# Attention of a hybrid decoder step on one core: TensorE in program order, two transpose banks, projections bank by bank at their ends

## The chip, the cores and the metric

The kernel runs on one core of one Trainium2 chip. The metric is the device time of one execution in microseconds (us), from the first to the last instruction with what lies around it; the median of several executions is quoted. Inside a core five engines work side by side, each through its own list of instructions in a fixed order: TensorE (PE, with its weight loads as PEld), VectorE (DVE), ScalarE (ACT), GpSimd (POOL) and SyncE (SP), which here only issues transfers. They wait for one another through semaphores. Matmul results land in PSUM, which has eight banks of 128 x 512 floats.

## The reference

One inference step of a two-layer trunk: 1024 prompt tokens and 8 sample tokens (1032 columns in the kernel), model width 1024. Layer 0 is a recurrent block, layer 1 is sliding-window attention, and each is followed by a squared-ReLU MLP of width 4096. The change lies in layer 1:

```python
def qkv_heads(x, w_qkv, q_g, k_g):
    q, k, v = jnp.split(x @ w_qkv, [Q_DIM, Q_DIM + KV_DIM], axis=-1)   # 16 query heads, 4 key/value heads of 64
    q = rms_norm(q.reshape(n, t, N_KV, GROUP, HEAD_DIM), q_g)
    k = rms_norm(k.reshape(n, t, N_KV, HEAD_DIM), k_g)
    ...
def sink_attention(q, k, v, dist, mask, sinks):
    s = jnp.einsum('...qkgd,...skd->...kgqs', q, k).astype(jnp.float32) * (HEAD_DIM ** -0.5)
    s = s - alibi_slopes()[:, :, None, None] * dist.astype(jnp.float32)
    s = jnp.where(mask, s, NEG_INF)
    m = jnp.maximum(jnp.max(s, axis=-1, keepdims=True), sink)
    e = jnp.exp(s - m)
    p = e / (jnp.sum(e, axis=-1, keepdims=True) + jnp.exp(sink - m))
    return jnp.einsum('...kgqs,...skd->...qkgd', p.astype(v.dtype), v)
```

Each block of 128 queries sees its own block of 128 keys and the one before it; there are 8 blocks.

## The kernel before

**Numbers.** Every large product is made from three passes: a float is split into a high and a low part (`wh`, `wl` for weights, `hh`, `hl` for activations), and high x high, high x low and low x high are added in the same bank. A split is one copy on ACT and one subtraction on DVE. The 1032 columns are worked in three chunks (344 each for k, 384, 384 and 264 for q).

**Attention.** Before the steps start, `proj_many` makes k and q of the first tile and `v_proj` makes v. The other seven q tiles and the second k tile are made by `filler`, a generator that runs between attention steps: one projection (`proj_steps`, L820) is 8 contractions x 3 passes x 3 chunks = 72 matmuls into three banks called P, one bank per chunk, with a pause (a `yield`) after every three. When the sums are complete, `q_take` (L777) reads each bank: a square on ACT (L782), a scaled copy on ACT (L783) and the low part on DVE (L784). After that `q_stats` (L791) sums the squares over each head with tiny matmuls of 2 columns (L798) into bank N and works the factors out of them (`factors_of`, L768 to L773: three small operations on ACT, three on DVE, the last of which still reads the bank). For k it is `k_evac` with `qk_norm` (L754): one 344-wide matmul per chunk (L757) into bank N, then three ACT and two DVE operations of 344 columns, of which the fourth (L315) still reads the bank.

**A step.** There are 32 steps: two query tiles (t0, t0+1; each tile holds two heads) for one block b. `stage_a` (L875) makes the scores: bias on POOL (L897, 4 operations), 12 matmuls into the two banks S (L904), then on DVE scores plus bias (L910, 4), on ACT the exponentials (L913, 4), the reciprocal on DVE (L915) and the scaling on POOL (L918, 4). `stage_b` (L921) turns the probabilities around with 8 transposes on TensorE, four per tile, into bank T (L928), which ACT copies out (L929). `stage_c` (L934) multiplies by v into bank O (L944). `stage_a` runs two steps ahead of `stage_b`, and `stage_c` one behind. From step 22 on (`J0`) the first contractions of the output projection (`entry_steps`, helper line L245) are the work between the steps, and the rest of that projection follows the last step.

**Banks.** P has three, S two, and T, O and N one each. A bank is given out again when the last reader of its tile is done.

**What sets the order.** The order on every engine is fixed when the program is built: a scheduler takes the instructions as written, estimates when each is ready, and places them; so on TensorE a matmul of a projection can come to stand between two of a score group. `tc.issue_after(x)` forces what follows behind x.

Of the kernel before, what the change touches and what calls it, by code (L numbers as in the profile page):

```python
# [64 lines left out]
def trunk(ctx: ExitStack, tc: tile.TileContext, I, O):  # L65
# [13 lines left out]
    def swap_banks(name):  # L79
        open_banks.close()  # L80
        psum["pool"] = open_banks.enter_context(tc.tile_pool(name=name, bufs=8, space=PSUM, reuse_waits="tile"))
# [32 lines left out]
    def B(tag=None):  # L114
        if tag is None:
            tag = ring[turn[0] % len(ring)]
            turn[0] += 1
        return psum["pool"].tile([P, 512], F32, tag=tag, bufs=BANKS[tag], name=nm("b" + tag))
# [120 lines left out]

    def mm_steps(outs, w, xs, chunks, col=lambda k: k * P, ks=None):  # L240
        nk = len(xs)
        for k in ks or range(nk):
            for a, (wt, xt) in enumerate(passes(w if isinstance(w, tuple) else w[k], xs[k])):
                for o, c in zip(outs, chunks):
                    last["mm"] = pe.matmul(o, lhsT=r_(wt[:, col(k):col(k) + P]), rhs=r_(xt[:, cs(c)]),  # L245
                                           start=(k == 0 and a == 0), stop=(k == nk - 1 and a == 2)).ins
            yield
# [146 lines left out]
    def out_proj(name, srcs, xsrc, gname, r, spill, **kw):  # L394
        xs, ws = [], []

        def need(n):
            while len(ws) < n:
                m = len(ws)
                ws.append(unit(name, m, 0))  # L400
                xs.append(A("x"))
                sp.dma_start(xs[m], xsrc[m])

        rs["tok"] = xs
        return xs, need, entry_steps(lambda m: ws[m], srcs, xs, gname, r, spill, **kw)
# [323 lines left out]
    def attention(hs):  # L729

        qg = cp.tile([P, 1], F32, name="qg")
# [22 lines left out]
        def qk_norm(sx, gcol):  # L754
            s, x = sx
            st = B("N")[:, :CH]
            pe.matmul(st, lhsT=blk, rhs=s, start=True, stop=True)  # L757
            r = rstd_m2(st)
            dve.scalar_tensor_tensor(x, x, gcol, r, ALU.mult, ALU.mult)
            return x  # L760
# [32 lines left out]
        def q_stats(t, c, s, part=False):  # L793
            if c == 0 or part:
                stq[t] = B("N")
            lo, hi = 3 * c, min(3 * c + 3, NB)
            for b in range(lo, hi):
                pe.matmul(stq[t][:, 2 * b:2 * b + 2], lhsT=s[:, (b - lo) * P:(b - lo) * P + P], rhs=halves, start=True, stop=True)  # L798
            if c == 2 or part:
                sl = slice(2 * lo if part else 0, 2 * hi)  # L800
                y, x = (fac[t % 4][:, 2 * NB * k:2 * NB * k + 2 * NB][:, sl] for k in range(2))
                factors_of(y, x, stq.pop(t)[:, sl], tmp[:, sl])
# [18 lines left out]
        def proj_steps(tag, w, cols, take, evac):  # L821
            ps = [B("P")[:, :sl.stop - sl.start] for sl in cols]
            for k in range(M8):
                for a, (wt, xt) in enumerate(passes(w, hs[k])):
                    for c, sl in enumerate(cols):
                        pe.matmul(ps[c], lhsT=r_(wt[:, k * P:k * P + P]), rhs=r_(xt[:, sl]),  # L826
                                  start=(k == 0 and a == 0), stop=(k == M8 - 1 and a == 2))
                    yield
            sx = [take(c, o) for c, o in enumerate(ps)]
            yield  # L830
            for c in range(NCH):
                evac(c, sx[c])
                yield
            done.add(tag)
# [49 lines left out]
        def stage_a(j):  # L884
# [16 lines left out]
            for t in (t0, t0 + 1):  # L901
                for a, (x, y) in enumerate(passes(kst[p], qs[t])):
                    for u, h in enumerate((lower, upper)):
                        pe.matmul(ss[u][:, (t - t0) * 256:(t - t0) * 256 + n], lhsT=r_(y[h, b * P:b * P + P]), rhs=r_(x[h, k0:k0 + n]),  # L904
                                  start=(a == 0), stop=(a == 2))
# [14 lines left out]
        def stage_b(j):  # L920
# [3 lines left out]
            for t in range(2):  # L924
                pt = B("T").rearrange("p (h u q) -> p h u q", h=2, u=2)
                for h in range(first, 2):
                    for u in range(2):
                        pe.transpose(pt[:, h, u, :], se[:, t, u, h * P:h * P + P], ident)  # L928
# [3 lines left out]
        def stage_c(j):  # L932
# [9 lines left out]
            for h in range(first, 2):  # L942
                for u, half in enumerate((lower, upper)):
                    pe.matmul(op[half, (b % 2) * 256:(b % 2) * 256 + 256], lhsT=vblk(b - 1 + h, t0 // 4, u),  # L944
# [88 lines left out]
        def filler():  # L1033
            for t in range(1, 8):
                if t == 4:
                    yield from proj_steps(("k", 1), unit("k", 1, 1), KCOLS, lambda c, o: take_out(o), lambda *a: k_evac(1, *a))
                yield from proj_steps(("q", t), unit("q", t, 1 if t < 7 else 0), QCOLS, lambda *a, t=t: q_take(t, *a),
                                      lambda *a, t=t: q_stats(t, *a))
# [6 lines left out]
        def between(m, c):  # L1045
            if c < 0 or (m, c) == (3, 0):
                need(m + 1)
# [28 lines left out]

        for j in range(AHEAD):
# [3 lines left out]
        for j in range(NJ):  # L1081
# [18 lines left out]
            if J0 - 1 <= j < J0 + 3:  # L1100
# [6 lines left out]
        stage_c(NJ - 1)  # L1107
        for t in range(6):
# [415 lines left out]
```

## Time and profile before

| | |
|---|---|
| median of 3 executions | 2036.92 us (2032.41 to 2039.14) |
| the profiled execution | 2030.05 us, of which the span from first to last instruction is 2028.3 us |
| granted TensorE clock, mean | 0.998 |
| busy share: PE, PEld, DVE, ACT, POOL | 99%, 96%, 68%, 52%, 18% |
| chain that ended last | PE 88%, DVE 4%, DMA 3%, issue 2%, ACT 2%, POOL 1% |
| attention steps | from about 1041.6 us (last of v) to about 1278 us; the rest of the output projection to about 1363 us |

"Busy" of PE is modelled from the starts, and a matmul that starts late still counts as busy; so the pace of TensorE is read from the distance between starts in the timeline, not from its busy share. The profile's lines are those of the kernel before. A matmul on plain floats (the v products of a step, the statistics) that stands once in the program shows as two in the trace.

### The profile page before, as it was taken

The numbers are of one execution on the slowest core, as the hardware profiler recorded it, in microseconds if no ns is written. First come the engines' busy times: TensorE is split into PE (matmuls) and PEld (weight loads), VectorE is DVE, ScalarE is ACT, GpSimd is POOL, SyncE is SP. The second block draws the span as 40 slices with busy tenths as digits, with TensorE's granted clock in tenths as the row PEclk, the third lists the DMA queues.
The fourth block names the chain that finished last, engine by engine and source line by source line (L and its number), as shares of the span: only waits on it lengthen the run. The fifth ranks groups of instructions, "written<-read, shape, count | busy, mean of one in ns | idle before, by whom it ended". The sixth has DMA issues, their size and how long they took to land.

```text
span 2028.3 us, 38515 instructions
## 1 busy us (share of the span) xinstructions
PE 2016.1 (99%) x15324; PEld 1955.3 (96%) x15324; DVE 1374.6 (68%) x2510; ACT 1058.9 (52%) x2073; POOL 365.8 (18%) x651
## 2 busy tenths in 40 slices
PE   9999999999999999999999999999999999999999
PEld 9999999999999999999998886999999999999999
DVE  7986639866666777766834537578766668776664
ACT  7786436444444555545536657455444436554551
POOL 2230100000002223321016548000000002332220
PEclk9999999999999999999999999999999999999999
DMA  5112412534346677877200003522443445887775
GB/s 179 41 43 63 166 61 67 172 136 152 136 152 243 163 218 207 224 203 204 83 26 22 23 12 116 179 77 106 142 163 120 168 138 179 222 218 197 206 195 134
DMA packets 99573, 281.68 MB, mean 139 GB/s; under 512 B 16184, under 2 KB 32192, under 8 KB 99392
## 3 DMA queue, kind: packets, MB, share of 16 engines
q0 software_dynamic: 28832, 97.32, 18.6%
q1 hardware_dynamic: 42624, 113.65, 17.9%
q10 hardware_dynamic: 27936, 68.23, 9.3%
q8 instruction: 120, 1.97, 0.4%
q14 instruction: 61, 0.50, 0.1%
HBM read 170.97 MB, written 108.19 MB: 138 GB/s over the span
## 4 chain that ended last, share of the span: by engine, by line
PE 88%; DVE 4%; DMA 3%; issue 2%; ACT 2%; POOL 1%; ACTq 0%; SPq 0%; DVEq 0%; POOLq 0%
PE bD L546 54%; PE bP L245 10%; PE bS L245 6%; PE bP L826 5%; PE bT L245 3%; PE bO L245 3%; DMA tl<-hsum 3%; PE bO L944 1%; PE bS L904 1%; PE bT L928 1%; PE bS L853 1%; DVE tl L420 1%; PE bN L798 1%; DVE op L414 1%; DVE xc L1231 0%
## 5 line engine op out<-in xcount | busy, mean ns | idle before, releaser
L546 PE MATMUL bD<-op,op 128*128 128x258 f32 x5544 | 678.6, 284 | 0.7 <-DVE y L380 0.7
L546 PEld LDWEIGHTS bD<-op,op 128*128 128x128 f32 x5544 | 670.8, 190 | 6.1 <-ACT ho L675 4.7
L546 PE MATMUL bD<-tl,op 128*128 128x258 f32 x4704 | 581.6, 284 | 2.3 <-ACT ho L675 1.8
L546 PEld LDWEIGHTS bD<-tl,op 128*128 128x128 f32 x4704 | 570.6, 190 | 10.7 <-ACT ho L675 8.6
L560 POOL DMA_DIRECT2D tl<-hsum x196 | 119.7, 765 | 891.5 <-ACT op L413 416.6
L414 DVE TENSOR_TENSOR op<-ws,op 128x384 fp32r<-128x384 f32 (+2 forms) x288 | 172.1, 606 | 109.2 <-ACT op L413 109.2
L675 ACT COPY he<-bD 128x516 f32<-128x516 f32 x144 | 84.8, 590 | 262.9 <-PE bD L546 262.8
L413 ACT CAST op<-ws 128x384 fp32r<-128x384 f32 (+2 forms) x288 | 158.3, 555 | 118.9 <-PE bD L546 76.4
L675 ACT COPY ho<-bD 128x516 f32<-128x516 f32 x144 | 84.8, 589 | 183.0 <-PE bD L546 178.6
L420 DVE TENSOR_TENSOR tl<-tl 128x516 fp32r<-128x516 f32 x196 | 129.9, 691 | 72.6 <-ACT tl L419 72.4
L413 ACT CAST op<-raw 128x384 fp32r<-128x384 f32 (+2 forms) x216 | 115.9, 555 | 44.1 <-PE bD L546 19.7
L414 DVE TENSOR_TENSOR op<-raw,op 128x384 fp32r<-128x384 f32 (+2 forms) x216 | 126.7, 603 | 5.9 <-ACT op L413 2.7
L419 ACT CAST tl<-tl 128x516 fp32r<-128x516 f32 x196 | 116.4, 626 | 22.3 <-DMA tl<-hsum 20.4
L683 DVE TENSOR_TENSOR ho<-bD,ho 128x516 f32<-128x516 f32 x72 | 49.9, 693 | 96.7 <-PE bD L546 96.7
L910 DVE CUSTOM_DVE_ANT_0 se<-bS,bias,nsink 128x256 f32<-128x256 f32 (+1 forms) x128 | 61.3, 525 | 37.0 <-PE bS L904 31.0
L694 POOL DMA_DIRECT2D spill<-ho x32 | 29.0, 906 | 293.4 <-DVE ho L683 290.8
L913 ACT ACTIVATE se<-se,den 128x257 f32<-128x257 f32 (+1 forms) x128 | 62.4, 491 | 37.3 <-DVE den L910 33.3
L186 DVE TENSOR_TENSOR wl<-raw,wh 128x1024 fp32r<-128x1024 f32 (+1 forms) x54 | 63.8, 1189 | 24.7 <-ACT wh L185 18.4
L897 POOL TENSOR_SCALAR bias<-con,fac 128x256 f32<-128x256 f32 (+1 forms) x128 | 63.9, 502 | 81.2 <-DVE den L910 51.6
L679 DVE TENSOR_TENSOR ho<-bD,ho 128x516 f32<-128x516 f32 x72 | 49.7, 690 | 39.6 <-ACT ho L675 39.6
L296 ACT ACTIVATE sq<-y 128x344 f32<-128x344 f32 x48 | 23.6, 492 | 77.1 <-DVE y L380 62.3
L677 DVE TENSOR_TENSOR he<-bD,he 128x516 f32<-128x516 f32 x72 | 49.7, 690 | 20.8 <-PE bD L546 15.3
(390 smaller groups left out, 3708.7 us busy)
## 6 DMA issues: line engine op xcount, KB each, us to landing
tl<-hsum POOLq DMA_DIRECT2D x196, 258.0 KB, 8.8
raw<-w_up SPq DMA_DIRECT2D x64, 512.0 KB, 4.2
raw<-w_dn SPq DMA_DIRECT2D x72, 384.0 KB, 6.3
spill<-he POOLq DMA_DIRECT2D x32, 516.0 KB, 9.0
spill<-ho POOLq DMA_DIRECT2D x32, 516.0 KB, 6.7
hsum<-ho ACTq DMA_DIRECT2D x28, 516.0 KB, 2.7
hsum<-he ACTq DMA_DIRECT2D x28, 516.0 KB, 2.7
hsum<-ts ACTq DMA_DIRECT2D x28, 516.0 KB, 2.9
```

Of the source, the lines that this page charges most:

```text
L186: eng.tensor_tensor(r_(lo[:, sl]), raw[:, sl], hi[:, sl], ALU.subtract)
L245: last["mm"] = pe.matmul(o, lhsT=r_(wt[:, col(k):col(k) + P]), rhs=r_(xt[:, cs(c)]), start=(k == 0 and a == 0), stop=(k == nk - 1 and a == ...
L413: act.copy(r_(t[:, 0:n]), src)
L414: dve.tensor_tensor(r_(t[:, n:2 * n]), src, t[:, 0:n], ALU.subtract)
L419: act.copy(r_(hi), lo)
L420: dve.tensor_tensor(r_(lo), lo, hi, ALU.subtract)
L546: ins = pe.matmul(d[:, 512 * b:512 * b + QT], lhsT=r_(wt[:, j * P:j * P + P]), rhs=r_(xt[:, QT * b:QT * b + QT]), start=first and j == 0 a ...
L560: pool.dma_start(t[:, n:2 * n], src)
L675: last["copy"] = act.copy(t, f).ins
L826: pe.matmul(ps[c], lhsT=r_(wt[:, k * P:k * P + P]), rhs=r_(xt[:, sl]), start=(k == 0 and a == 0), stop=(k == M8 - 1 and a == 2))
L897: pool.tensor_scalar(bias(t, u), distM[:, 256 - n:256], fac[t % 4][:, 2 * NB + 2 * b + u:2 * NB + 2 * b + u + 1], 0.25 * SLOPES[head(t, u) ...
L913: act.activation(e[:, 256 - n:257], e[:, 256 - n:257], AF.Exp, scale=-1.0, bias=dn[:, o:o + 1], accum_out=dn[:, 4 + o:5 + o])
```

## The change

Four things are done, all in attention:

- Every matmul of the step loop goes through a helper `chain`. While a switch `strict` is on (from the first step to the last), it forces each one behind the one issued before it, so TensorE runs in the order in which the program is written.
- For attention a bank pool of its own is opened. In it bank N is gone, and T has two banks, which transposes and statistics share.
- A projection runs its first two and its last two contractions one bank after the other (6 matmuls into the first bank, 6 into the second, 6 into the third), and the four contractions between as before. Its banks are read as each is complete. The statistics of a projection are issued together, after the ninth pause of the next projection. A projection now has 24 pauses and one more for the statistics, where it had 28; how many pauses a step takes is left as it was.
- The output projection's residual rows are fetched later (when its first tile is finished, not when its early contractions begin), and one early weight load is left out of the step loop, to come when it is asked for.

```diff
     def swap_banks(name):
         open_banks.close()
+        psum["pair"] = name == "pa"
...
+        if psum["pair"] and tag in ("N", "T"):
+            return psum["pool"].tile([P, 512], F32, tag="T", bufs=2, name=nm("bT"))
         return psum["pool"].tile([P, 512], F32, tag=tag, bufs=BANKS[tag], name=nm("b" + tag))
...
+    strict = [False]
+
+    def chain(op, *a, **kw):
+        with ExitStack() as s:
+            if strict[0]:
+                s.enter_context(tc.issue_after(last["pe"]))
+            r = op(*a, **kw)
+        last["pe"] = r.ins
+        return r
...
-        def need(n):
+        def need(n, weights=False):
             while len(ws) < n:
-                m = len(ws)
-                ws.append(unit(name, m, 0))
+                ws.append(unit(name, len(ws), 0))
+            while len(xs) < n and not weights:
                 xs.append(A("x"))
-                sp.dma_start(xs[m], xsrc[m])
+                sp.dma_start(xs[-1], xsrc[len(xs) - 1])
...
     def attention(hs):
 
+        swap_banks("pa")
...
-            pe.matmul(st, lhsT=blk, rhs=s, start=True, stop=True)
+            chain(pe.matmul, st, lhsT=blk, rhs=s, start=True, stop=True)
...
-        def proj_steps(tag, w, cols, take, evac):
+        def proj_steps(w, cols, take, sx):
             ps = [B("P")[:, :sl.stop - sl.start] for sl in cols]
-            for k in range(M8):
-                for a, (wt, xt) in enumerate(passes(w, hs[k])):
-                    for c, sl in enumerate(cols):
-                        pe.matmul(ps[c], lhsT=r_(wt[:, k * P:k * P + P]), rhs=r_(xt[:, sl]),
-                                  start=(k == 0 and a == 0), stop=(k == M8 - 1 and a == 2))
+
+            def mm(k, a, c):
+                wt, xt = passes(w, hs[k])[a]
+                chain(pe.matmul, ps[c], lhsT=r_(wt[:, k * P:k * P + P]), rhs=r_(xt[:, cols[c]]),
+                      start=(k == 0 and a == 0), stop=(k == M8 - 1 and a == 2))
+
+            def by_chunk(ks):
+                for c in range(NCH):
+                    for k in ks:
+                        for a in range(3):
+                            mm(k, a, c)
+                        yield c, k
+
+            for _ in by_chunk((0, 1)):
+                yield
+            for k in range(2, M8 - 2):
+                for a in range(3):
+                    for c in range(NCH):
+                        mm(k, a, c)
                     yield
-            sx = [take(c, o) for c, o in enumerate(ps)]
-            yield
-            for c in range(NCH):
-                evac(c, sx[c])
+            for c, k in by_chunk((M8 - 2, M8 - 1)):
+                if k == M8 - 1:
+                    sx.append(take(c, ps[c]))
                 yield
-            done.add(tag)
...
         def filler():
-            for t in range(1, 8):
-                if t == 4:
-                    yield from proj_steps(("k", 1), unit("k", 1, 1), KCOLS, lambda c, o: take_out(o), lambda *a: k_evac(1, *a))
-                yield from proj_steps(("q", t), unit("q", t, 1 if t < 7 else 0), QCOLS, lambda *a, t=t: q_take(t, *a),
-                                      lambda *a, t=t: q_stats(t, *a))
+            late = None
+
+            def finish():
+                tag, evac, sx = late
+                for c in range(NCH):
+                    evac(c, sx[c])
+                done.add(tag)
+
+            for tag in [("q", 1), ("q", 2), ("q", 3), ("k", 1)] + [("q", t) for t in range(4, 8)]:
+                n, t = tag
+                sx = []
+                if n == "k":
+                    cols, grab, evac = KCOLS, lambda c, o: take_out(o), lambda *a: k_evac(1, *a)
+                else:
+                    cols, grab, evac = QCOLS, lambda *a, t=t: q_take(t, *a), lambda *a, t=t: q_stats(t, *a)
+                for i, _ in enumerate(proj_steps(unit(n, t, 1 if tag != ("q", 7) else 0), cols, grab, sx)):
+                    yield
+                    if i == 8 and late:
+                        finish()
+                        yield
+                late = tag, evac, sx
+            yield
+            finish()
...
         def between(m, c):
-            if c < 0 or (m, c) == (3, 0):
-                need(m + 1)
+            if c < 0:
+                need(m + 1, True)
+            if (m, c) in ((0, 0), (3, 0)):
+                need(max(m + 1, 3))
...
+        strict[0] = True
         for j in range(AHEAD):
...
-            if J0 - 1 <= j < J0 + 3:
+            if J0 - 1 <= j < J0 + 2:
                 ensure(index["wo1", j - J0 + 1])
...
         stage_c(NJ - 1)
+        strict[0] = False
```

Three places of the program show the order before and after. In the names, `bP` is a projection bank, `bT` a transpose bank, `bN` the statistics bank, `bS` and `bO` scores and outputs; `se` holds probabilities, `pt` turned ones, `sq` squares; `x4` is four in a row.

TensorE before, the two groups of transposes of one step, around the middle of a projection:

```order
L826 MATMUL bP_12530<-hl_10770,wh_12258 128x344
L928 MATMUL bT_12664<-con,se_11365 128x128 x4
L826 MATMUL bP_12528<-hh_10769,wl_12259 128x344
L826 MATMUL bP_12529<-hh_10769,wl_12259 128x344
L826 MATMUL bP_12530<-hh_10769,wl_12259 128x344
L826 MATMUL bP_12528<-hh_10771,wh_12258 128x344
L826 MATMUL bP_12529<-hh_10771,wh_12258 128x344
L928 MATMUL bT_12670<-con,se_11365 128x128 x4
L826 MATMUL bP_12530<-hh_10771,wh_12258 128x344
```

TensorE now, the same place of a later step:

```order
L249 MATMUL bP_12968<-hl_10764,wh_12711 128x264
L249 MATMUL bP_12968<-hh_10763,wl_12712 128x264
L249 MATMUL bT_13027<-con,se_11369 128x128 x4
L249 MATMUL bT_13033<-con,se_11369 128x128 x4
L249 MATMUL bP_12966<-hh_10765,wh_12711 128x384
L249 MATMUL bP_12967<-hh_10765,wh_12711 128x384
```

The two groups stand together, in two different banks, and the projection's matmuls stand around them.

TensorE before, the first of the three statistics matmuls of the second k tile (`bN_12772`; the other two follow 38 and 53 rows later):

```order
L826 MATMUL bP_12530<-hh_10775,wl_12259 128x344
L944 MATMUL bO_12812<-pt_12663,v_11362 64x256
L928 MATMUL bT_12749<-con,se_11366 128x128 x4
L757 MATMUL bN_12772<-sq_12758,con 128x344
L944 MATMUL bO_12812<-pt_12663,v_11362 64x256 x3
L904 MATMUL bS_12817<-kh_11415,qh_12212 128x256
```

TensorE now, all three, between a score group and a projection:

```order
L249 MATMUL bS_12765<-kl_11420,qh_12380 128x256
L249 MATMUL bT_12799<-sq_12647,con 128x344
L249 MATMUL bT_12811<-sq_12657,con 128x344
L249 MATMUL bT_12823<-sq_12667,con 128x344
L249 MATMUL bP_12715<-hh_10767,wh_12449 128x384
```

The three stand in a row. There are two banks T, so the third (`bT_12823`) gets the bank of the first, and the transposes nine projection matmuls later (`bT_12849`, `bT_12855`) get those of the second and the third.

ScalarE now, at the same place (`se` rows are the exponentials of the score group just before):

```order
L939 ACTIVATE se_11369,den_11357<-se_11369,den_11357 128x257
L325 ACTIVATE q_12802<-bT_12799,vec 128x344
L939 ACTIVATE se_11369,den_11357<-se_11369,den_11357 128x257 x3
L326 ACTIVATE r_12801<-q_12802 128x344
L325 ACTIVATE q_12814<-bT_12811,vec 128x344
L327 ACTIVATE q_12802<-r_12801 128x344
L326 ACTIVATE r_12813<-q_12814 128x344
L327 ACTIVATE q_12814<-r_12813 128x344
L289 CAST kh_12797<-x_12648 128x344
L325 ACTIVATE q_12826<-bT_12823,vec 128x344
```

The chain that frees the first bank (L325, L326, L327, then one operation on DVE) has four exponentials and one operation of the second chunk among it.

More of the change, by code (lines that the diff above doesn't have):

```diff
@@ L244, in mm_steps @@
                 for o, c in zip(outs, chunks):
-                    last["mm"] = pe.matmul(o, lhsT=r_(wt[:, col(k):col(k) + P]), rhs=r_(xt[:, cs(c)]),
-                                           start=(k == 0 and a == 0), stop=(k == nk - 1 and a == 2)).ins
+                    last["mm"] = chain(pe.matmul, o, lhsT=r_(wt[:, col(k):col(k) + P]), rhs=r_(xt[:, cs(c)]),
+                                       start=(k == 0 and a == 0), stop=(k == nk - 1 and a == 2)).ins
             yield
@@ L797, in q_stats @@
             for b in range(lo, hi):
-                pe.matmul(stq[t][:, 2 * b:2 * b + 2], lhsT=s[:, (b - lo) * P:(b - lo) * P + P], rhs=halves, start=True, stop=True)
+                chain(pe.matmul, stq[t][:, 2 * b:2 * b + 2], lhsT=s[:, (b - lo) * P:(b - lo) * P + P], rhs=halves, start=True, stop=True)
             if c == 2 or part:
@@ L903, in stage_a @@
                     for u, h in enumerate((lower, upper)):
-                        pe.matmul(ss[u][:, (t - t0) * 256:(t - t0) * 256 + n], lhsT=r_(y[h, b * P:b * P + P]), rhs=r_(x[h, k0:k0 + n]),
+                        chain(pe.matmul, ss[u][:, (t - t0) * 256:(t - t0) * 256 + n], lhsT=r_(y[h, b * P:b * P + P]), rhs=r_(x[h, k0:k0 + n]),
                                   start=(a == 0), stop=(a == 2))
@@ L927, in stage_b @@
                     for u in range(2):
-                        pe.transpose(pt[:, h, u, :], se[:, t, u, h * P:h * P + P], ident)
+                        chain(pe.transpose, pt[:, h, u, :], se[:, t, u, h * P:h * P + P], ident)
                 (dve.tensor_copy if t and t0 == 6 else act.copy)(pw[:, first:, :, t, :], pt[:, first:])
@@ L943, in stage_c @@
                 for u, half in enumerate((lower, upper)):
-                    pe.matmul(op[half, (b % 2) * 256:(b % 2) * 256 + 256], lhsT=vblk(b - 1 + h, t0 // 4, u),
+                    chain(pe.matmul, op[half, (b % 2) * 256:(b % 2) * 256 + 256], lhsT=vblk(b - 1 + h, t0 // 4, u),
                               rhs=pw[:, h, u, :, :].rearrange("p t q -> p (t q)"), start=(h == first), stop=(h == 1))
```

## The prediction

> **What bounds the kernel now.** I read the engines' totals first, then three stretches of attention, then TensorE's timeline inside them. The totals:
>
> ```profile
> PE 2016.1 (99%) x15324; PEld 1955.3 (96%) x15324; DVE 1374.6 (68%) x2510; ACT 1058.9 (52%) x2073; POOL 365.8 (18%) x651
> ```
>
> TensorE is never idle for long, but this share says nothing of its pace: a late matmul counts as busy. The stretches (length; busy time and count of PE, PEld, DVE, ACT, POOL; granted clock; DMA share; GB/s) are the projection ahead of the steps, the first to the 24th score group, and the rest of the steps:
>
> ```profile
> core 0: us, PE busy (x) PEld busy (x) DVE busy (x) ACT busy (x) POOL busy (x), PEclk, DMA share, GB/s
> 1041.60:1053.00 11.40, 11.40 (x75) 11.21 (x74) 0.00 (x0) 0.57 (x2) 0.94 (x3) 1.00 0.01 3
> 1053.00:1223.50 170.50, 170.23 (x1204) 142.18 (x1203) 81.24 (x310) 101.95 (x319) 90.45 (x204) 0.98 0.06 17
> 1223.50:1278.00 54.50, 51.12 (x378) 36.96 (x378) 40.21 (x127) 39.78 (x118) 39.51 (x82) 1.00 0.34 118
> ```
>
> In the middle stretch no other engine is busy for more than 102 of 170.5 us, so TensorE's list sets the time there. What its work should cost is read from starts (start, busy, line):
>
> ```profile
> 1113.02 0.60 PE L928 MATMUL bT<-con,se 128*128 128x128 f32 x4
> 1113.37 0.71 PE L826 MATMUL bP<-hh,wl 128*128 128x344 f32 x3
> 1113.92 0.48 PE L826 MATMUL bP<-hh,wh 128*128 128x344 f32 x2
> 1114.38 0.63 PE L928 MATMUL bT<-con,se 128*128 128x128 f32 x4
> ...
> 1115.95 0.64 PE L826 MATMUL bP<-hh,wh 128*128 128x344 f32 x3
> 1116.52 1.08 PE L944 MATMUL bO<-pt,v 128*64 128x256 f32 x8
> 1117.54 0.39 PE L904 MATMUL bS<-kh,qh 64*128 64x256 f32 x2
> ...
> 1118.44 0.74 PE L826 MATMUL bP<-hl,wh 128*128 128x344 f32 x3
> 1119.01 0.63 PE L826 MATMUL bP<-hh,wl 128*128 128x344 f32 x3
> 1119.48 0.64 PE L826 MATMUL bP<-hh,wh 128*128 128x344 f32 x3
> ```
>
> Three projection matmuls take 0.47 us (1119.01 to 1119.48): 0.157 each. Four transposes take 0.35, and the three matmuls behind them 0.55 (1113.37 to 1113.92), so a group costs 0.43. Eight output matmuls take 1.02, and the three ahead of them 0.57: 1.12 in all. A score group takes 0.90, and 0.10 more at the matmuls behind it: 1.00. And the two matmuls at 1113.92 take 0.46 where 0.31 would do: the second transposes wait 0.15 us for the one bank T.
>
> The middle stretch also has places where the scheduler cut groups up with the statistics matmuls (L798):
>
> ```profile
> 1170.00:1180.00 10.00, 10.00 (x55) 8.79 (x56) 3.50 (x17) 3.73 (x14) 4.21 (x11) 0.83 0.16 52
> 1169.11 0.83 PE L798 MATMUL bN<-con,sq 128*128 128x2 f32 x6
> 1169.87 0.32 PE L904 MATMUL bS<-kh,qh 64*128 64x128 f32 x1
> 1170.13 0.83 PE L798 MATMUL bN<-con,sq 128*128 128x2 f32 x6
> ...
> 1175.20 1.06 PE L826 MATMUL bP<-hh,wl 128*128 128x384 f32 x3
> 1176.06 1.06 PE L826 MATMUL bP<-hh,wh 128*128 128x384 f32 x3
> ```
>
> Single score matmuls stand between statistics, and the granted clock falls (mean 0.83 over 10 us, which is 1.7 us lost): three matmuls then take 0.86 us (1175.20 to 1176.06). It falls once more at the first such place:
>
> ```profile
> 1050.00:1060.00 10.00, 9.97 (x58) 8.85 (x57) 3.33 (x13) 4.08 (x13) 1.45 (x4) 0.88 0.00 0
> ```
>
> 0.12 of 10 us is 1.2 us. In the last stretch another engine sets the pace:
>
> ```profile
> 1249.31 1.84 POOL L918 TENSOR_SCALAR se<-se,den 128x256 f32<-128x256 f32 x4
> 1251.24 1.95 POOL L897 TENSOR_SCALAR bias<-con,fac 128x256 f32<-128x256 f32 x4
> ...
> 1255.23 1.95 POOL L897 TENSOR_SCALAR bias<-con,fac 128x256 f32<-128x256 f32 x4
> ```
>
> POOL's bias and scaling follow each other without a gap, 3.99 us from one step's bias to the next (1251.24 to 1255.23), while TensorE's own work for a step without a projection is 0.90 + 2 x 0.43 + 1.12 = 2.9 us.
>
> **The change part by part.** *What grouping and the second bank T remove.* The program's order before holds, between the first and the 24th score group, 504 projection matmuls, 23 score groups, 39 groups of transposes, 18.5 groups of eight output matmuls, 7 sets of statistics (16 matmuls each in the trace) and the 3 matmuls of the k norm. The prices of the last two come from the rows below: 0.114 per statistics matmul, 1.8 per set; 0.7 per k norm matmul (an estimate from the 0.85 busy of its row, which overlaps the next). So 504 x 0.157 + 23 x 1.00 + 39 x 0.43 + 18.5 x 1.12 + 7 x 1.8 + 3 x 0.7 = 154.3 us, and the stretch took 170.5: 16.2 us are cuts, waits and 2.9 us of slow clock. Grouping can take away all of it at most.
>
> In the new order 99 projection matmuls and one set stand ahead of the first score group, where it was 72: it comes at 1041.6 + 11.4 + 27 x 0.157 + 1.8 = 1059.0. The projections are used up sooner too, since a projection has 25 pauses instead of 28 and a step takes as many pauses as before: the last ones stand ahead of the 21st score group, not the 24th. From the first to the 21st there are 477 projection matmuls, 20 score groups, 33 groups of transposes, 15.5 of outputs, 6 sets, 3 k norm matmuls: 74.9 + 20.0 + 14.2 + 17.4 + 10.8 + 2.1 = 139.4. Without any wait the 21st would come at 1198.4.
>
> *What the strict order adds.* A matmul whose bank is not free now holds back all that stands behind it on TensorE; before, the scheduler had put other work there. The places where the list shows it are those where statistics and transposes meet in two banks. The k norm:
>
> ```profile
> 1129.19 0.85 PE L757 MATMUL bN<-sq,con 128*128 128x344 f32 x2
> 1130.07 0.55 ACT L312 ACTIVATE q<-bN,vec 128x344 f32<-128x344 f32 x1 [1.29 <-PE bN L757]
> 1131.53 0.50 ACT L314 ACTIVATE q<-r 128x344 f32<-128x344 f32 x1
> 1132.06 0.57 DVE L315 SCALAR_TENSOR_TENSOR q<-bN,vec,q 128x344 f32<-128x344 f32 x1 [0.51 <-ACT q L314]
> 1132.69 0.85 PE L757 MATMUL bN<-sq,con 128*128 128x344 f32 x2
> ```
>
> One use of the bank lasts 3.5 us (1129.19 to 1132.69), and the next matmul starts as L315 ends (1132.63). In the new order the third matmul needs the first one's bank and is due 2 x 0.7 = 1.4 us after it. At the least it waits 3.5 - 1.4 = 2.1 us. But ScalarE's new list has four exponentials and an operation of the second chunk inside this chain. Exponentials follow at 0.49 us:
>
> ```profile
> 1149.44 0.50 ACT L913 ACTIVATE se<-se,den 128x257 f32<-128x257 f32 x1
> 1149.93 0.50 ACT L913 ACTIVATE se<-se,den 128x257 f32<-128x257 f32 x1
> ```
>
> The first can start about 0.8 us after the score group; with four at 0.49, four 344-wide operations at 0.4 (an estimate: they are 0.50 to 0.55 long, and the next starts inside) and L315's 0.57, the bank is free at 5.0: a wait of 3.6. The third matmul's bank goes to the second group of transposes; its chain ends about 4.1 us after its start (two casts of the finished k stand among it on ScalarE), while only 0.7 + 9 x 0.157 + 0.43 = 2.6 us of work lie between: 1.5 more. I take 5.1, from 2.1 to 6.
>
> A set of statistics (`factors_of`):
>
> ```profile
> 1147.45 1.28 PE L798 MATMUL bN<-con,sq 128*128 128x2 f32 x10
> 1148.59 0.60 PE L826 MATMUL bP<-hh,wh 128*128 128x384 f32 x2
> 1148.76 0.28 ACT L768 ACTIVATE tmp<-bN,vec 128x16 f32<-128x16 f32 x1 [0.33 <-PE bN L798]
> 1152.32 0.23 DVE L773 SCALAR_TENSOR_TENSOR fac<-bN,vec,fac 128x16 f32<-128x16 f32 x1
> ```
>
> Ten take 1.14 us, and the bank is held 3.96 us past the last (1148.59 to 1152.55), here with other work among the chain; six short operations alone would take about 1.7 (an estimate at 0.28 each, the length of the first). In two of the six sets the list has the second group of transposes 0.9 and 0.4 us behind it (three projection matmuls and the first group; the first group alone): it waits 0.8 and 1.3 at least, 3.1 and 3.6 at most. With the exponentials that ScalarE's list puts ahead there I take 2.1 and 1.9. In two more the set follows eight transposes directly and waits for the copy of their first bank behind four exponentials: 0.8 + 4 x 0.49 + about 0.5 = 3.2 us after the score group, due at 0.10 + 12 x 0.157 + 2 x 0.43 = 2.8: 0.4 each. Together 4.8, from 2.1 to 8.7.
>
> *Bank by bank.* Between the end of a projection's first bank and the next one's first matmul lie 12 matmuls, 1.9 us. Reading a bank out takes 1.6 us (the square's start to the end of the low part at 1145.77):
>
> ```profile
> 1144.17 0.48 ACT L782 ACTIVATE sq<-bP 128x384 f32<-128x384 f32 x1
> 1145.15 0.62 DVE L784 SCALAR_TENSOR_TENSOR ql<-bP,qg,qh 128x384 fp32r<-128x384 f32 x1 [1.15 <-ACT qh L783]
> ```
>
> So the 12 matmuls hide it, and in most places a group of scores, transposes or outputs lies between as well. Where exponentials stand ahead on ScalarE a few tenths show: 0.5 in all, up to 3 if that cover is gone at all seven edges.
>
> *The clock.* The k norm's wait is 3.6 us of nothing, and a set with a wait behind it some 4 us of little. The two rows at 0.83 and 0.88 show that much less than an idle TensorE costs 1.2 to 1.7 us each. I take one such fall, 1.7; none to three are possible.
>
> *The end of the steps.* Steps 21 to 23 lose their projections and fall to POOL's pace: 3 x 4.0 = 12.0 us. The output projection's early contractions fill the same later steps as before. Its residual rows are asked for later, but still before the 13 us of contractions that follow the last step; one such transfer lands in 2.7 to 9 us on other queues
>
> ```profile
> spill<-he POOLq DMA_DIRECT2D x32, 516.0 KB, 9.0
> hsum<-ho ACTq DMA_DIRECT2D x28, 516.0 KB, 2.7
> ```
>
> and DMA is at 0.34 in that stretch: nothing; if it were exposed, some 3 us. Leaving one early weight load out: nothing, it comes when its tile is asked for, a step later.
>
> *The sum.* 1198.4 + 5.1 + 4.8 + 0.5 + 1.7 = 1210.5 for the 21st score group, + 12.0 = 1222.5 for the 24th, which came at 1223.5. Behind it the work is the same, and the output projection and the MLP follow at TensorE's pace. So the span falls by 1.0 us: 2029 for the profiled execution's 2030.05. That execution lies 6.9 us under the median of 2036.92, so the forecast for the median is 2036. What is won at the cuts (13.3 and one slow clock) is spent on banks and on steps without filler.
>
> **The rivals.** *Faster: the waits stay at their short ends.* For it: the chains alone need 3.5 and 1.7 us, and ScalarE is busy for only 102 of 170.5 us, so the exponentials may be done in time. Against it: its list is fixed, with the exponentials ahead. The waits would be 2.1 + 2.1 = 4.2 in place of 10.4, without a slow clock: 7.9 us less, 2021 profiled, 2028 median.
>
> *Slower: statistics block the transposes, and the idle stretches cost the clock.* Every set's bank is held for its 3.96 us: 3.1 + 3.6 + 2 x 1.0 + 6 for the k norm + 0.5, and three falls of 1.7: 20.3 in place of 12.1, 8.2 more, 2037 profiled, 2044 median. It decides from about 18 us of waits on. For it: the clock fell twice without any idle time. Against: the longest holds have other work in them that need not be there.
> The Trainium skill (TensorE: Matmul & The Clock Gate, Part 1) says that a free-running window of about 3.4 us is judged by how busy TensorE was, and that an idle one is followed by half speed. By that rule the k norm's wait alone can cost one fall of 1.7 us, as in the sum; the rows at 0.83 and 0.88 agree with the size and fall sooner than an idle window.
>
> *Slower: the last steps are longer than POOL's 4.0.* With the transposes and outputs of a step in front of the next scores, a late copy holds the scores back. 0.75 us on each of the 11 steps from the 21st score group is 8.2 us: 2037, 2044 median. Against: TensorE has 1.1 us to spare in each.
>
> That the order stays as it was is ruled out by the lists.
>
> **How the numbers follow.** The forecast has 0.42 (its own range 2030 to 2042), the faster rival 0.32, the slower ones 0.16 and 0.10. A difference under 0.3%, 6.1 us, cannot be told from none. The faster rival at 2028 is past that bound nearly always, the slower ones at 2044 mostly, and a little of the forecast lies beyond it on each side: 0.32 faster, 0.43 the same, 0.25 slower. The range runs from the faster rival with some of its waits gone as well to the slower ones: 2023 to 2047.
>
> **What would show it.** In the new profile: eight transposes together in about 0.8 us with no wait between the two groups, and steps of 7.2 us with 27 projection matmuls, show the gain. A gap of 3 to 4 us ahead of the third k norm matmul, gaps of about 2 us between two groups of transposes behind a set of statistics, and a clock under 0.9 there show the price. Three steps of 4.0 us without projections ahead of the early contractions show the filler's end. If the gaps are under 1 us, the time is nearer 2028; if steps late in the list exceed 5 us, nearer 2044.

## The result, and the profile after

The changed kernel takes 2054.44 us (median of 6 executions, 2052.66 to 2058.16) against 2036.35 for the kernel before (6 executions on the same chip): a ratio of 1.0092 with a 95% interval of 1.0078 to 1.0106. It is 18 us slower. The forecast, 2036 us in a range from 2023 to 2047, was wrong.

The profiled execution of the changed kernel took 2055.89 us. It differs from the one of before by 25.8 us in the span; the medians differ by less, since before's profiled execution was 6 us faster than its median. In the 84 executions of before that ran beside the experiments the time goes with the granted clock (2029.9 to 2032.7 us at 0.998, 2033.6 to 2038.0 at 0.996, 2040.4 to 2041.8 at 0.993), so before's profile, at 0.998, shows fewer slow stretches than is usual for that kernel. The engines' totals of the changed kernel:

```profile
PE 2016.6 (98%) x15324; PEld 1961.1 (95%) x15324; DVE 1377.5 (67%) x2510; ACT 1060.2 (52%) x2073; POOL 358.8 (17%) x651
```

TensorE has the same number of matmuls and almost the same busy time, so the totals say nothing. The places of the program do. The rows are split at starts on TensorE; "block" is the first uninterrupted run of over 50 projection matmuls of the step loop, "forecast" is the prediction's own working:

| stretch (us) | before | forecast | after |
|---|---|---|---|
| start to the MLP's last down matmul | 988.3 | 988.3 | 990.4 |
| to the first block | 53.3 | 53.3 | 68.1 |
| to the first score group | 11.4 | 17.4 | 18.3 |
| to the 21st score group | | 151.5 | 156.8 |
| to the 24th | 170.5 for both | 12.0 | 9.9 |
| to the last output matmul of attention | 53.9 | 53.9 | 53.8 |
| to the end | 750.9 | 750.9 | 756.8 |

So 14.8 of the 25.8 us come between the MLP and the step loop, and 5.9 after it. The 2.1 us of the first row cannot be told from spread: that stretch took 988.2 us in before and 990.0 in e2 below, and 990.4 in the changed kernel, 988.7 in e4 and 989.8 in e12. Two windows at the end of the MLP (length; busy time and count of PE, PEld, DVE, ACT, POOL; granted clock; DMA share; GB/s), before:

```profile
988.00:1000.00 12.00, 12.00 (x75) 12.00 (x74) 9.40 (x19) 7.55 (x16) 0.00 (x0) 1.00 0.42 130
1000.00:1010.00 10.00, 10.00 (x67) 9.59 (x66) 9.61 (x19) 5.17 (x12) 0.00 (x0) 1.00 0.23 75
```

and after:

```profile
988.00:1000.00 12.00, 3.76 (x19) 3.11 (x19) 11.51 (x24) 7.81 (x16) 0.00 (x0) 0.78 0.27 89
1000.00:1010.00 10.00, 7.87 (x36) 7.58 (x36) 7.58 (x15) 5.59 (x11) 0.00 (x0) 0.75 0.38 123
```

TensorE idles for 8.2 of 12 us, and the clock is at 0.78 and 0.75 of full speed. TensorE's timeline of before shows what filled this place (start, busy, line, output<-inputs; `hd` are the operands of the MLP's last down products, `hh` and `hl` those of attention's projections):

```profile
988.24 0.32 PE L245 MATMUL bS<-hdh,wl 128*128 128x344 f32 x1
988.39 0.32 PE L245 MATMUL bS<-hh,wh 128*128 128x344 f32 x1
...
996.55 0.32 PE L245 MATMUL bO<-hl,wh 128*128 128x344 f32 x1
996.71 0.32 PE L285 MATMUL bN<-shi,ones 128*128 128x344 f32 x1
996.87 0.32 PE L245 MATMUL bO<-hh,wl 128*128 128x344 f32 x1
```

The first k and q projections follow the last down matmul at once, and the sum of squares for the MLP's last norm (L285) slips in among them when ScalarE and VectorE have it ready. After (L298 is the same sum):

```profile
990.35 0.32 PE L249 MATMUL bS<-hdh,wl 128*128 128x344 f32 x1
998.51 0.66 PE L298 MATMUL bN<-shi,ones 128*128 128x344 f32 x1 [7.84 <-ACT shi L296]
999.57 0.66 PE L299 MATMUL bN<-slo,ones 128*128 128x344 f32 x1 [0.40 <-DVE slo L297]
1000.02 0.49 PE L249 MATMUL bS<-hh,wh 128*128 128x344 f32 x1
1000.30 0.49 PE L249 MATMUL bS<-hl,wh 128*128 128x344 f32 x1
```

Now the sum is first in TensorE's list, with nothing in front of it for 7.84 us, and the projections start 9.7 us behind the last down matmul, at half clock (0.28 us from one to the next where it was 0.16).

Inside the loop the strict order's waits are listed between the first block and the 24th score group (what waited and for what; us in total, times, longest):

```profile
PE bT L249 <- DVE q L328: 4.4, 2, 3.8
PE bP L249 <- DVE ql L798: 2.9, 4, 1.4
PE bT L249 <- ACT fac L783: 1.2, 1, 1.2
PE bT L249 <- ACT pt L955: 1.1, 2, 0.6
PE bT L249 <- ACT tmp L784: 1.0, 1, 1.0
PE bP L249 <- DVE aux L802: 0.2, 1, 0.2
```

And from the first score group on, stretch by stretch, the granted clock (seventh figure behind the window):

```profile
1076.80:1233.63 156.83, 146.58 (x1078) 127.04 (x1077) 72.88 (x275) 90.56 (x283) 76.77 (x182) 0.97 0.05 15
1233.63:1243.56 9.93, 9.82 (x88) 6.65 (x86) 7.46 (x31) 8.45 (x30) 7.85 (x18) 1.00 0.01 2
1243.56:1297.40 53.84, 48.66 (x371) 36.98 (x369) 38.42 (x124) 39.18 (x117) 39.83 (x86) 0.94 0.34 114
1297.40:1360.00 62.60, 62.57 (x389) 62.09 (x386) 32.02 (x85) 25.73 (x58) 0.00 (x0) 0.92 0.45 152
```

The share that is missing from 1.00, times the length, is 4.7, 3.2 and 5.0 us; with 2.6 and 2.5 from the two windows at 988 to 1010 it makes 18 us of slow clock, where this execution of before had 3. Part of it lies where TensorE was idle anyway. The 5.9 us behind the loop are mostly that 5.0: before has 1.00 there.

```profile
1277.50:1340.00 62.50, 62.49 (x418) 61.93 (x415) 33.99 (x89) 27.67 (x61) 0.00 (x0) 1.00 0.46 151
```

That this 5.0 is a cost of the change is not shown. e1 and e12 below differ only in where the pool is opened, and between about 1282 and 1360 us the granted clock is 1.00 in e1's trace and 0.91 in e12's.

### The profile page after: what moved, and what is told of

It is laid out like the page before. It is cut to its first block, busy times and chain, and to the rows that moved or that the text cites. A ratio compares the mean times of both kernels' runs of the same rounds, so it can differ in the third digit from the quotient of the medians.

```text
span 2054.1 us, 38524 instructions
## 1 busy us (share of the span) xinstructions
PE 2016.6 (98%) x15324; PEld 1961.1 (95%) x15324; DVE 1377.5 (67%) x2510; ACT 1060.2 (52%) x2073; POOL 358.8 (17%) x651
## 3 DMA queue, kind: packets, MB, share of 16 engines
q0 software_dynamic: 28832, 97.32, 18.3%
## 4 chain that ended last, share of the span: by engine, by line
PE 85%; DVE 6%; ACT 3%; DMA 3%; issue 3%; POOL 0%; ACTq 0%; SPq 0%; DVEq 0%; POOLq 0%
PE bD L559 54%; PE bP L249 13%; PE bS L249 7%; PE bT L249 5%; PE bO L249 4%; DMA tl<-hsum 2%; DVE op L427 1%; ACT se L939 1%; PE bS L879 1%; DVE tl L433 1%; DVE xc L1279 0%; DVE wl L189 0%; DVE ws L527 0%; ACT wh L188 0%; DMA x<-xT 0%
## 5 line engine op out<-in xcount | busy, mean ns | idle before, releaser
L249 PE MATMUL bP<-hh,wh 128*128 128x344 f32 (+2 forms) x368 | 111.4, 331 | 3.8 <-DVE ql L798 2.9
L249 PE MATMUL bP<-hh,wl 128*128 128x344 f32 (+2 forms) x368 | 109.2, 325 | 0.1
L249 PE MATMUL bP<-hl,wh 128*128 128x344 f32 (+2 forms) x368 | 108.9, 325 | 0.0
```

The lines of the kernel that those rows point to most:

```text
L249: r = op(*a, **kw)
```

## The experiments

"No new pool" below means that attention opens no banks of its own. Medians of before in the four groups of runs were 2036.1 to 2037.2 us. The ratios compare with before in the same group; they differ from the quotient of the two medians by up to 0.0005, which is 1 us.

### Where the first 14 us come from

**e1, the change without the new pool.**

```diff
-        psum["pair"] = name == "pa"
+        psum["pair"] = name == "pd0"
...
-        swap_banks("pa")
```

> The changed kernel, but attention opens no banks of its own: the pair of T banks is there from the last layer-0 MLP stage on. Pool theory: the new pool keeps the first k and q projections behind the last norm of the MLP (14.6 us between 988 and the first projection block in the two profiles), so about 14 us come back: 2054.4 - 14 = about 2040 us, and the projection block starts near 1043 us as before. Rival (TensorE's strict order, with its waits and clock falls, costs the 18 us): about 2054 us.

Measured: 2038.21 us, ratio 1.0007 (0.9994 to 1.0021). The first block comes 54.1 us behind the last down matmul. The pool theory holds.

**e2, the kernel before with a new pool.**

```diff
     def attention(hs):
+        swap_banks("pa")
```

> The kernel before with one line more: attention opens a new bank pool with the same tags and sizes; nothing else. Pool theory: 2036.4 + 14 = about 2050 us, with TensorE idle at 990 to 1000 us and its clock at half there. Rival (strict order or the shared pair costs the time): within 2 us of 2036.4.

Measured: 2049.60 us, ratio 1.0059 (1.0040 to 1.0078). One line that changes no computation costs 12 us, in the same place:

```profile
988.00:1000.00 12.00, 3.76 (x19) 3.11 (x18) 11.12 (x23) 7.57 (x17) 0.00 (x0) 0.78 0.29 102
...
998.12 0.65 PE L285 MATMUL bN<-shi,ones 128*128 128x344 f32 x1 [7.84 <-ACT shi L283]
```

**e12, the change with its pool opened later.**

```diff
-        swap_banks("pa")
         qg = cp.tile([P, 1], F32, name="qg")
...
         v_proj()
+        swap_banks("pa")
```

> The changed kernel (strict, pair), with its own bank pool opened behind the v projections instead of at attention's start. Theory that a new pool's banks are handed out only behind the old pool's last work: the 14 us at the MLP's end go (54 us from the last down projection to the first projection block instead of 68), and the new place costs little, since only projections stand ahead of it: 2054.4 - 14 = about 2040 us. Rival that a new pool costs its 14 us wherever it is opened: 2054.

Measured: 2037.63 us, ratio 1.0010 (0.9997 to 1.0024): the 14 us are gone (53.3 us to the first block). A new pool costs nothing that can be measured where all that stands ahead of it is due first anyway:

```profile
988.00:1000.00 12.00, 12.00 (x75) 12.00 (x74) 10.99 (x23) 7.57 (x17) 0.00 (x0) 1.00 0.31 101
```

The waiting matmul is itself late for ScalarE, not for a bank, and what could go ahead of it stands behind it in the list. So the pool acts when the order is fixed: tiles of the new pool are placed behind the last tile of the old one. That this is the rule by which the scheduler goes is argued from the three lists; its inside was not looked at.

### What the strict order costs, and what earns it

**e4, the change with its new pool, not strict.**

```diff
-        strict[0] = True
+        strict[0] = False
```

> The changed kernel with its new pool and pair, bank-by-bank projections and moved calls, but TensorE's order left to the planner's priorities. Pool theory: the 14 us at attention's start remain, about 2050 us. Strict-order rival: about 2036 to 2040 us.

Measured: 2036.35 us, ratio 0.9994 (0.9983 to 1.0005), and 68.1 us to the first block. My number, 2050, was wrong: the pool's 14 us are there, yet from the first block to the last output matmul the loop takes 222.2 us, against 238.8 in the change and 235.8 before. So the strict order costs 18 us too (2054.4 - 2036.4), and something else in the change earns 14.

**e5, the two costs taken out: no new pool, and not strict.**

```diff
-        psum["pair"] = name == "pa"
+        psum["pair"] = name == "pd0"
...
-        swap_banks("pa")
...
-        strict[0] = True
+        strict[0] = False
```

> The changed kernel without its two costs as the first four runs show them: no new pool (the pair from the MLP stage on) and TensorE's order left to the planner; pair and bank-by-bank projections stay. If the two costs add: 2036.4 of the run without strict order less the 13.5 us that the pool cost there (68.1 against 54.1 from the last down projection to the first projection block) = about 2023 us. Rival (the free order gained only because TensorE had stood late): 2036.

Measured: 2021.46 us, ratio 0.9933 (0.9920 to 0.9945): the costs add, and what is left of the change is 15 us faster than before.

**e6, the kernel before with the pair of T banks only; e7, the change without pool, pair and strict order.** These split the gain.

```diff
+        psum["pair"] = name == "pd0"
...
+        if psum["pair"] and tag in ("N", "T"):
+            return psum["pool"].tile([P, 512], F32, tag="T", bufs=2, name=nm("bT"))
```

> The kernel before with N and T as a pair of shared banks from the last layer-0 MLP stage on, and nothing else. Theory that the pair gives the gain (the free order has 224 runs of one kind of matmul then, 266 before): a good half of 13 us, about 2028. Rival that bank-by-bank projections with late statistics give it: 2036.

```diff
-        psum["pair"] = name == "pa"
+        psum["pair"] = False
...
-        swap_banks("pa")
...
-        strict[0] = True
+        strict[0] = False
```

> The changed kernel with separate banks as before, no new pool, order left to the planner: what remains is the projections' bank-by-bank ends, the later statistics and the moved calls (239 runs of one kind against 266). Theory that the pair gives the gain: about 2034. Rival that these projections give it: about 2024.

Measured: e6 2035.43 us, ratio 1.0001 (0.9992 to 1.0010); e7 2029.15, ratio 0.9967 (0.9958 to 0.9977). e6 came out at its rival's 2036, e7 between its two numbers, so neither part gives the gain by itself. The pair alone gives nothing, the projections' new form alone 7 us, both together 15. In the loop's list the runs of one kind of matmul fall from 266 (before) to 224 (e6), 239 (e7) and 184 (e5): the two take away different cuts. Which of the cuts is worth what was not settled.

**e3, the change without pool and pair, strict.**

```diff
-        psum["pair"] = name == "pa"
+        psum["pair"] = False
...
-        swap_banks("pa")
```

> The changed kernel with the banks of the kernel before (one N, one T, no new pool): the strict order and the bank-by-bank projections remain. Pool theory: about 2040 us, as without the new pool, plus up to 0.8 us a step for the second transpose group that waits for its bank again (24 steps: up to 19 us): 2040 to 2059. Rival that strict order costs the 18 us: 2054 or more. Rival that the pair, by sharing banks with the statistics, costs time: below 2040.

Measured: 2080.86 us, ratio 1.0211 (1.0186 to 1.0236), 44 us slower than before and far past the 2059 that the pool theory allowed; of the expectations only the rival's open "2054 or more" covers it. With one T bank the second transposes of each step wait, and in strict order nothing goes ahead of them. Its largest waits:

```profile
PE bT L249 <- ACT pt L954: 31.7, 24, 2.6
PE bN L249 <- DVE q L328: 6.4, 2, 4.1
PE bT L249 <- POOL se L943: 6.1, 3, 3.7
```

The pair is worth 43 us to the strict order, 8 to the free one (e7 against e5).

### Which part of the strict order

**e8, e1 with the statistics out of the strict order.**

```diff
-            chain(pe.matmul, st, lhsT=blk, rhs=s, start=True, stop=True)
+            pe.matmul(st, lhsT=blk, rhs=s, start=True, stop=True)
...
-                chain(pe.matmul, stq[t][:, 2 * b:2 * b + 2], ...
+                pe.matmul(stq[t][:, 2 * b:2 * b + 2], ...
```

> The changed kernel without the new pool, in strict order, but with the statistics matmuls (q sets, k norm) outside the strict order. Theory that these hold the strict order up (k norm 4.2 us, transposes behind the q sets 4.5 us, and the clock falls that follow them, 5 us): 2038.2 - 9 to 14 = 2024 to 2029. Rival that strict order costs at the edges of projections and at the first output projections (P 5.1 us, W 2.9 us): 2034 to 2038.

Measured: 2034.87 us, ratio 0.9992 (0.9983 to 1.0001). 3 of the 17 us between e1 and e5 (15 by their ratios); the theory fell. The step from the 10th score group to the 11th still takes 15.3 us.

**e9, e1 with earlier output weights; e10, e1 with the k norm in three pieces; e11, both.** These are aimed at the two longest single waits of e1's loop, 3.8 and 2.6 us:

```profile
PE bT L249 <- DVE q L328: 3.8, 1, 3.8
PE bP L249 <- DVE ql L797: 2.9, 4, 1.4
PE bP L249 <- ACT wh L188: 2.6, 1, 2.6
```

```diff
-            if J0 - 1 <= j < J0 + 2:
-                ensure(index["wo1", j - J0 + 1])
+            if J0 - 3 <= j < J0:
+                ensure(index["wo1", j - J0 + 3])
```

> The changed kernel without the new pool, strict; the first three units of output-projection weights are fetched and split three steps of stage_b earlier by two (at j = 19, 20, 21 instead of 21, 22, 23). Theory that the step from the 25th score group to the 26th (10.9 us strict, 5.2 free) waits for their split on ScalarE: it falls to 5.5, the clock fall at 1238 us goes with it, 2038.2 - 5.4 = about 2033 us. Rival that the split only moves onto the exponentials of an earlier step: 2038.

```diff
-                    if i == 8 and late:
+                    if late and late[0][0] == "k" and 8 <= i <= 12 and i % 2 == 0:
+                        late[1](i // 2 - 4, late[2][i // 2 - 4])
+                        if i == 12:
+                            done.add(late[0])
+                        yield
+                    elif i == 8 and late and late[0][0] == "q":
```

> The changed kernel without the new pool, strict; the three chunks of the second k norm are handed in two projection steps apart instead of in one piece. Theory that the step from the 10th score group to the 11th (14.9 us strict, 9.1 free) is the wait of the third norm matmul for a T bank and the clock fall behind it: it falls to about 9.5, 2038.2 - 5.4 = about 2033 us. Rival that the wait goes over to the transposes behind each norm matmul, since they share the two banks: 2037 or more.

> Both edits of the two runs before, strict, no new pool. If those two waits are the price of the strict order: 2038.2 - 11 = about 2027 us, still above the 2021.5 of the free order by the smaller waits (q sets, projection edges). Rival that strict order loses elsewhere what it gains here: 2033 or more.

Measured: e9 2035.24 us, ratio 0.9998 (0.9987 to 1.0009), the step fell from 10.9 to 6.0; e10 2037.06, ratio 1.0007 (0.9996 to 1.0019), the step fell from 14.9 to 12.9, e11 2031.58, ratio 0.9984 (0.9969 to 0.9999). e9's step fell as expected, yet the time by 3 us instead of 5; e10's time is its rival's. Together 5 to 7 us come back (by the ratios, by the medians), not 11. The rival of e10 was right in its reason too, at least in part: in e10, and in e11 as listed here, waits have gone over to the transposes.

```profile
PE bT L249 <- ACT pt L954: 3.8, 4, 2.0
PE bT L249 <- DVE q L328: 3.4, 2, 2.9
PE bP L249 <- DVE ql L797: 1.9, 2, 1.4
```

**e13, e1 with the projections out of the strict order; e14, e1 with scores, transposes and outputs out of it.**

```diff
-                    last["mm"] = chain(pe.matmul, o, ...
+                    last["mm"] = pe.matmul(o, ...
...
-                chain(pe.matmul, ps[c], ...
+                pe.matmul(ps[c], ...
```

e14 leaves these two as they are and takes `chain` off the matmuls of scores, transposes and outputs in the same way.

> The changed kernel without the new pool; scores, transposes, outputs and statistics stay in strict order among themselves, the projections (q, k and output) are free to fill. Theory that the cost of strict order is that no projection matmul can step into a wait: nearly all comes back, 2021 to 2026 us. Rival that attention's own groups held in order are the cost: 2032 or more.

> The changed kernel without the new pool; projections and statistics stay in strict order among themselves, scores, transposes and outputs are free. A projection can then step in front of a waiting transpose and the other way round, only the statistics still hold projections up. Theory of the missing filler: most comes back too, 2022 to 2028 us, with the statistics' waits left. Rival that projections in order are the cost (their edges, the output weights): 2032 or more.

Measured: e13 2018.82 us, ratio 0.9913 (0.9898 to 0.9928), the fastest of all and 18 us under before; e14 2024.67, ratio 0.9944 (0.9928 to 0.9961). So attention's own groups may stand in strict order at no cost (e13), and projections may stand in order among themselves at little (e14: 13 to 14 us come back). The cost lies in the tie between the two: when one of them waits, the other may not go ahead. Of the two, freeing the projections is worth 6 us more. The k norm shows it. The change, at the norm's third matmul:

```profile
1141.92 1.42 PE L249 MATMUL bT<-sq,con 128*128 128x344 f32 x4
1147.14 0.84 PE L249 MATMUL bT<-sq,con 128*128 128x344 f32 x2 [3.80 <-DVE q L328]
1147.57 0.94 PE L249 MATMUL bP<-hh,wh 128*128 128x384 f32 x3
```

e13, the same place (the projections are L839 there):

```profile
1123.22 1.42 PE L249 MATMUL bT<-sq,con 128*128 128x344 f32 x4
1124.22 0.89 PE L839 MATMUL bP<-hh,wh 128*128 128x384 f32 x3
...
1128.45 0.85 PE L249 MATMUL bT<-sq,con 128*128 128x344 f32 x2
```

The third norm matmul waits for its bank as long as before, but 25 projection matmuls go ahead of it. What e13 still waits for between 1040 and 1290 us is 2.4 us, where e1 listed some 15:

```profile
PE bT L249 <- ACT fac L782: 1.2, 1, 1.2
PE bT L249 <- ACT pt L954: 0.9, 2, 0.8
PE bP L258 <- DVE wl L189: 0.3, 1, 0.3
```

e14 still has 5.4 us in the same list, the largest entry at the k norm, which there still holds the projections:

```profile
PE bT L249 <- DVE q L328: 1.9, 1, 1.9
PE bT L953 <- POOL bias L922: 0.9, 2, 0.8
```

**e15, e5 with the earlier weights of e9.**

```diff
-            if J0 - 1 <= j < J0 + 2:
-                ensure(index["wo1", j - J0 + 1])
+            if J0 - 3 <= j < J0:
+                ensure(index["wo1", j - J0 + 3])
```

> The fastest kernel so far (pair, bank-by-bank projections, no new pool, free order: 2021.5 us) with the output projection's first weights split two steps earlier. Theory that their wait is the strict order's: no change, 2019.5 to 2023.5 us (its profile shows 0.7 us of waiting for them). Rival that the split is late there too and the free order only covers it with other late work: 2018 or less.

Measured: 2021.23 us, ratio 0.9922 (0.9904 to 0.9940): no change from e5. The long wait for those weights was the strict order's: 2.6 us in e1's list, 0.7 in e5's.

## Why the prediction was wrong

**The step that failed first** is "it comes at 1041.6 + 11.4 + 27 x 0.157 + 1.8 = 1059.0". The 17.4 us behind 1041.6 measured 18.3, but 1041.6 itself was taken over from before. The change opens a pool at attention's start, and the prediction costed the two T banks in it and not its opening: no line is said of the projections that had stood across the border between MLP and attention. e1, e2 and e12 show 14 us there: the first block comes 67.6 to 68.1 us behind the last down matmul with the early pool and 53.3 to 54.1 without it. The list of TensorE at each place where the change opens something, not only in the loop, was the thing to read.

**The waits of the strict order** were named rightly, and without the pool the total (e1: 2038.21) is 2 us from the forecast. Part of that nearness is luck: in e1's trace the loop took 5.0 us more than forecast up to the 21st score group and 2.1 less from there to the 24th. Term by term, in the changed kernel to the 21st score group: the third k norm matmul waits 3.8 us (forecast 3.6); the transposes behind the norm 0.6 (1.5); the sets of statistics 3.3, the rows `fac`, `pt` and `tmp` together (4.8); the banks' edges 3.1, the rows `ql` and `aux` (0.5, with 3 as the end "if that cover is gone"); the clock 4.7 (1.7). The clock and the edges were mis-sized. The three clock falls of the first slower rival were there in this stretch (at 1121, 1148 and 1217 us), without its long holds.

**The steps without filler** were right in kind: three steps took 9.9 us, not 12.0. POOL is busy for 7.85 us of them and ScalarE for 8.45 (the row from 1233.63), so POOL did not set their pace.

**"Behind it the work is the same"** was right on the work, and to the last output matmul on the time too (53.8 us, forecast 53.9), though not for the stated reason: a wait of 2.6 us for the output projection's weights (L188 in e1's list) is new there, and so is a clock fall behind it, and what made up for them was not traced. e9, which loads these weights earlier, takes the wait away. The remainder of the output projection has two clock falls that before's profile had not; since e1's has none there either, they are not shown to be the change's.

**"What is won at the cuts"**, the forecast had, "is spent on banks and on steps without filler". On the banks that is what happened: 14 to 15 us won (e5 against before), 15 to 17 spent (e1 against e5), each by ratios and by medians. The prediction took the trade as given; e13 shows it is not, since the groups can be kept in order while the projections stay free.

That the change does what it says held: eight transposes stand together at 0.79 us a group and a full step takes 7.2 us, as forecast:

```profile
1126.61 0.39 PE L249 MATMUL bS<-kh,qh 64*128 64x256 f32 x2
...
1129.52 1.03 PE L249 MATMUL bT<-con,se 128*128 128x128 f32 x8
1130.31 0.40 PE L249 MATMUL bP<-hh,wh 128*128 128x344 f32 x1
...
1133.85 0.33 PE L249 MATMUL bS<-kh,qh 64*128 64x128 f32 x2
```

## What to carry to other kernels

Before costing the inside of a change, follow the engine's list across the borders of the stage that it touches: a resource that is opened anew can order work that used to overlap there (12 to 17 us here for one line). Fix the order of the work whose order matters and leave the long, independent filler free: groups in order with free projections gave 2018.8 us, projections in order with free groups 2024.7, all in order 2038.2, all free 2021.5. Two edits that each look worth nothing or half (0 and 7 us) can be worth 15 together, so a split by parts needs the pairs too.

## What was not expected of the hardware

**The clock falls after a window with few columns, not only after an idle one.** In all 17 traces the falls of the granted clock last 3.41 us or a multiple of it (up to 10.24), those at the program's very end apart, and start on a grid of that step. I laid the grid over 900 to 1400 us of each trace and summed the columns that the matmuls of each window stream, at 0.157 us per 344 (a projection matmul's pace), as a share of the window. Of the windows at full clock, the following one was slow:

| share of the window that streams columns | windows | followed by half clock |
|---|---|---|
| under 0.25 | 27 | 26 |
| 0.25 to 0.35 | 27 | 15 |
| 0.35 to 0.50 | 108 | 18 |
| 0.50 and more | 2209 | 0 |

The columns are my measure; what the chip itself counts is not shown, and between 0.25 and 0.50 this measure does not decide. A fall needs no idle time: in the kernel before this window has TensorE busy throughout, 10 of its 22 matmuls being statistics of two columns, and the next one is at half speed.

```profile
1170.34:1173.75 3.41, 3.41 (x22) 0.99 0.35 137
1173.75:1177.16 3.41, 3.41 (x14) 0.51 0.00 0
```

The Trainium skill (TensorE: Matmul & The Clock Gate, Part 1) puts the fall behind at least one idle window of about 3.4 us; the length of the window agrees, the condition does not: of the 59 falls, 24 follow a window in which the profile has TensorE busy throughout, and only 3 one in which it was idle throughout. Where the grid lies over the program differs from trace to trace. That this is why falls behind the loop (starting between 1310 and 1370 us) are in some of these traces and absent from others is likely, but not shown.
